# Streaming the activations' high and low halves as one 512-column matmul in a float32 decoder block

## The chip, the cores and the metric

One core of one Trainium2 chip. The metric is device microseconds for one execution of the whole kernel, median over runs.

## The reference, cut to what matters

A decoder block on 256 tokens (S), width 1024 (D): an HGRN2 recurrence and an attention branch read one normalised input, their outputs are projected, gated, summed and projected again, and a SwiGLU FFN (width 2816) follows. All of it is float32.

```python
h = rmsnorm(x, attn_norm_g[l])
proj = h @ w_in[l]
hq, hf, hi, hg, aq, ak, av, gl = jnp.split(proj, IN_SPLITS, axis=-1)
y_hg = hgrn2_mix(hq, hf, hi, hg, lb_all[l], hg_out_norm_g[l]) @ w_branch_hg[l]
...
merged = gates[:, :, 0, :] * y_hg + gates[:, :, 1, :] * y_at
x = x + merged @ w_out[l]
h2 = rmsnorm(x, ffn_norm_g[l])
x = x + (jax.nn.silu(h2 @ w_ffn_gate[l]) * (h2 @ w_ffn_up[l])) @ w_ffn_down[l]
```

## The kernel before, in words

Every large product is done in split precision. A float32 operand becomes a high half in the `fp32r` type, made by a ScalarE copy (line 52), and a low half, the rest, made by a VectorE subtract (line 53); `split` holds the two. A product a x w is then three matmuls: high x high, high x low and low x high, summed in PSUM.

Weights come in parts of 4 k-tiles of 128 rows by 512 columns (1 MB): `load_w` (line 55) issues the DMA on SP's queue and splits what lands. Its three tiles `wraw`, `whi`, `wlo` have three buffers each.

Two helpers do the products with the 1024-wide input. `tok_block` (line 73) keeps the activations stationary and streams 512 weight columns, so tokens lie on partitions and two PSUM banks are used. `feat_block` (line 83) keeps a 128 x 128 weight block stationary and streams the 256 tokens, so features lie on partitions; for each part of 4 k-tiles it goes over 4 feature tiles `ct`, and for each over the 4 k-tiles, with three matmuls of 256 columns (lines 94 to 96). Two feature tiles share one bank of 512 float32 columns, so a block of 512 features takes two banks. Both helpers take their banks from the pool `pw`, which has four; `down` (line 561) accumulates the FFN's last product in four banks of the pools `ph` and `pa`.

In the order of the code: V0 (a token block, its matmuls in lines 137 to 139), F0 (a `feat_block` on columns 1024 to 1535 of `w_in`), then `rx` and `R` (the norm's reciprocal, from the input `xtok` by lines 195, 161, 162; `spread`, line 164, lays it over the partitions with the matmul of line 169), `put_tok(V, V0)` (line 206, empties V0's banks and scales by `rx`), F1, the position bias (line 238 to 257, with copies on POOL in line 253), Q0 and Q1 (`feat_block`, line 261). Then come token blocks for attention between the steps of the recurrence (`hgrn_level`, whose ScalarE copy `KP` in line 296 shares the buffer T15 with the bias' `Bx`), four `feat_block` of branch gates (line 506), two each on `w_at` and `w_hg` (lines 520, 524), a token block on `w_out`, and the FFN: for each 512 hidden features a gate block, an up block and the `down` of the features before.

The Tile framework orders the instructions of each engine when the kernel is built: among those that it holds ready it takes the one written earliest, so an instruction can overtake earlier ones that are not ready in its plan. On the chip each engine then runs in that fixed order. A tile of a pool is given to the next user once all readers of the last one are done.

Of the kernel before, what the change touches and what calls it, by code (L numbers as in the profile page):

```python
# [14 lines left out]
P = 128  # L15
# [3 lines left out]
H = 8  # L19
# [8 lines left out]
def tile_hgrn2_moba_block(ctx: ExitStack, tc: tile.TileContext, xm, xT, vecs, table, onehot,  # L28
# [21 lines left out]

    def split(src, hi, lo):
        nc.scalar.copy(hi, src)  # L52
        nc.vector.tensor_sub(lo, src, hi.bitcast(F32))  # L53
# [19 lines left out]
    def tok_block(w, c0, ah, al, parts=(4, 4)):  # L73
        ps = [pw(), pw()]
        for kt, wh, wl in chunks(w, c0, 512, parts):
            for tb in range(2):
                ts = slice(tb * P, (tb + 1) * P)
                nc.tensor.matmul(ps[tb], ah[:, kt, ts], wh, start=(kt == 0), stop=False)  # L78
                nc.tensor.matmul(ps[tb], ah[:, kt, ts], wl, start=False, stop=False)  # L79
                nc.tensor.matmul(ps[tb], al[:, kt, ts], wh, start=False, stop=(kt == KT - 1))  # L80
        return ps

    def feat_block(w, c0, ah, al, cw=512, parts=(4, 4), cut=1):
        n = cw // P
        ps = [pw() for _ in range(n // 2)]
        k = 0
        for pn in parts:
            hi, lo = load_w(w[k * P:(k + pn) * P, c0:c0 + cw].rearrange("(k p) c -> p k c", p=P), [pn, cw], cut)
            for ct in range(n):
                cs = slice(ct * P, (ct + 1) * P)  # L90
                o = ps[ct // 2].rearrange("p (a t) -> p a t", a=2)[:, ct % 2, :]
                for i in range(pn):
                    kt = k + i
                    nc.tensor.matmul(o, hi[:, i, cs], ah[:, kt, :], start=(kt == 0 and ct % 2 == 0), stop=False)  # L94
                    nc.tensor.matmul(o, hi[:, i, cs], al[:, kt, :], start=False, stop=False)  # L95
                    nc.tensor.matmul(o, lo[:, i, cs], ah[:, kt, :], start=False,  # L96
                                     stop=(kt == KT - 1 and ct % 2 == 1))
            k += pn
        return [p.rearrange("p (a t) -> p a t", a=2) for p in ps]
# [11 lines left out]
    XTh = big.tile([P, KT, S], F32R, name="XTh", tag="XH")  # L111
    XTl = big.tile([P, KT, S], F32R, name="XTl", tag="XL")
    V = big.tile([P, 2, D], F32, name="V", tag="T6")
    V0 = [pw(), pw()]
    for g, pieces in enumerate(((1, 1, 2), (2, 2))):
# [4 lines left out]
        for n in pieces:  # L120
# [6 lines left out]
            for kt in range(xs.start, xs.stop):  # L127
                nc.scalar.mul(XTh[:, kt, :], xTr[:, kt, :], vec[:, kt:kt + 1])
                nc.vector.scalar_tensor_tensor(XTl[:, kt, :], xTr[:, kt, :], vec[:, kt:kt + 1],
                                               XTh[:, kt, :].bitcast(F32), op0=OP.mult, op1=OP.subtract)  # L130
                if kt == xs.start:
                    split(raw[:, ks, :], wh[:, ks, :], wl[:, ks, :])
            for i in range(k0, k0 + n):
                kt = 4 * g + i
                for tb in range(2):
                    ts = slice(tb * P, (tb + 1) * P)
                    nc.tensor.matmul(V0[tb], XTh[:, kt, ts], wh[:, i, :], start=(kt == 0), stop=False)
                    nc.tensor.matmul(V0[tb], XTl[:, kt, ts], wh[:, i, :], start=False, stop=False)
                    nc.tensor.matmul(V0[tb], XTh[:, kt, ts], wl[:, i, :], start=False, stop=(kt == KT - 1))  # L139
# [48 lines left out]
    F0 = feat_block(w_in, 1024, XTh, XTl, cut=2)  # L188
# [22 lines left out]
    K = big.tile([P, 2, H, P], F32, name="K", tag="T2")  # L211
    Fg = big.tile([P, 2, H, P], F32, name="Fg", tag="T3")
    for half in range(2):
        ps = F0 if half == 0 else feat_block(w_in, 1024 + half * 512, XTh, XTl, cut=2 - half)
        for j in range(2):
# [3 lines left out]
            nc.vector.tensor_mul(fz, ps[j].rearrange("p h (b t) -> p h b t", b=2),  # L219
                                 Rb.rearrange("p h (b t) -> p h b t", b=2))  # L220
# [39 lines left out]
    for half in range(2):  # L260
        ps = feat_block(w_in, half * 512, XTh, XTl)
        for j in range(2):
            h = half * 4 + j * 2
            nc.vector.tensor_mul(Q[:, :, h:h + 2, :].rearrange("p b h t -> p h b t"),
                                 ps[j].rearrange("p h (b t) -> p h b t", b=2),
                                 Rqb.rearrange("p h (b t) -> p h b t", b=2))

# [89 lines left out]
    def hgrn_gate(o, ro, sg):  # L357
# [5 lines left out]
        oTh = big.tile([P, H, S], F32R, name="oTh", tag="T3")  # L363
        oTl = big.tile([P, H, S], F32R, name="oTl", tag="T4")
        for g in range(4):
# [6 lines left out]
            hi = oTh[:, 2 * g:2 * g + 2, :].rearrange("p h t -> p (h t)")  # L372
            lo = oTl[:, 2 * g:2 * g + 2, :].rearrange("p h t -> p (h t)")
            nc.scalar.mul(hi, bank, og)
            nc.vector.scalar_tensor_tensor(lo, bank, og, hi.bitcast(F32), op0=OP.mult, op1=OP.subtract)
        return oTh, oTl

# [1 line left out]
    def qk_block(tok, sq, c0, half):  # L379
        put_tok(tok, tok_block(w_in, c0 + half * 512, XTh, XTl), half)  # L380
# [66 lines left out]
    def values(Va, PT0, PT1):  # L447
        aTh = big.tile([P, H, S], F32R, name="aTh", tag="T7")
        aTl = big.tile([P, H, S], F32R, name="aTl", tag="T10")
        for g in range(4):  # L450
# [6 lines left out]
            gs = slice(2 * g, 2 * g + 2)  # L457
            split(bank, aTh[:, gs, :].rearrange("p h t -> p (h t)"), aTl[:, gs, :].rearrange("p h t -> p (h t)"))
        return aTh, aTl
# [15 lines left out]
    put_tok(V, tok_block(w_in, 2048 + 512, XTh, XTl), 1)  # L475
# [3 lines left out]
    put_tok(Va, tok_block(w_in, 6144, XTh, XTl), 0)  # L479
# [3 lines left out]
    put_tok(Va, tok_block(w_in, 6144 + 512, XTh, XTl), 1)  # L483
# [4 lines left out]
    def gate_block(half):  # L488
        ps = tok_block(w_in, 3072 + half * 512, XTh, XTl)
# [4 lines left out]
    aTh, aTl = values(Va, PT0, PT1)  # L494
# [6 lines left out]
    G = []  # L501
    for br in (1, 0):
        g_t = big.tile([P, KT, S], F32, name=f"G{br}", tag=("T5", "T6")[br])
        G.insert(0, g_t)
        for half in range(2):
            ps = feat_block(w_in, 7168 + br * D + half * 512, XTh, XTl)
            for j in range(2):
                g = g_t[:, half * 4 + 2 * j:half * 4 + 2 * j + 2, :]
                nc.vector.tensor_mul(g, ps[j], Rb)
                nc.scalar.activation(g, g, AF.Sigmoid)  # L510
            if br == 1 and half == 0:
                oTh, oTl = hgrn_gate(o, ro, sg)

# [1 line left out]
    Mh = big.tile([P, KT, S], F32R, name="Mh", tag="T8")  # L515
    Ml = big.tile([P, KT, S], F32R, name="Ml", tag="T9")
    x2 = big.tile([P, 2, D], F32, name="x2", tag="T1")
    nc.gpsimd.dma_start(x2, xm.rearrange("(b p) c -> p b c", p=P))
    for half in range(2):
        pa_ = feat_block(w_at, half * 512, aTh, aTl)  # L520
        for j in range(2):
            g = G[1][:, half * 4 + 2 * j:half * 4 + 2 * j + 2, :]
            nc.vector.tensor_mul(g, g, pa_[j])
        pb_ = feat_block(w_hg, half * 512, oTh, oTl)
        for j in range(2):
            ks = slice(half * 4 + 2 * j, half * 4 + 2 * j + 2)
            g = G[0][:, ks, :]
            nc.vector.tensor_mul(g, g, pb_[j])
            nc.vector.tensor_add(g, g, G[1][:, ks, :])
            split(g, Mh[:, ks, :], Ml[:, ks, :])  # L530

# [1 line left out]
    x2h = big.tile([P, KT, S], F32R, name="x2h", tag="XH")  # L533
    x2l = big.tile([P, KT, S], F32R, name="x2l", tag="XL")
    ss2 = small.tile([P, 2, 2], F32, name="ss2")
    for half in range(2):
        ps = tok_block(w_out, half * 512, Mh, Ml)
        for tb in range(2):
# [6 lines left out]
            ks = slice(half * 4, half * 4 + 4)  # L545
            nc.vector.tensor_mul(xg, bank.rearrange("p (k t) -> p k t", k=4),
                                 vec[:, 8 + half * 4:12 + half * 4].unsqueeze(2).to_broadcast([P, 4, P]))
            split(xg, x2h[:, ks, tb * P:(tb + 1) * P], x2l[:, ks, tb * P:(tb + 1) * P])
# [10 lines left out]
    acc = [[None, None], [None, None]]  # L559

    def down(f0, nf, act, last):
        ah, al = act
        for j0 in range(0, nf, 2):
            hi, lo = load_w(w_down[(f0 + j0) * P:(f0 + j0 + 2) * P, :].rearrange("(j p) c -> p j c", p=P), [2, D])
            end = last and j0 + 2 == nf
            for tb in range(2):
                for half in range(2):
                    ts = slice(tb * P, (tb + 1) * P)
                    cs = slice(half * 512, (half + 1) * 512)
                    for i in range(2):  # L570
# [3 lines left out]
                        nc.tensor.matmul(acc[tb][half], ah[:, j, ts], hi[:, i, cs], start=st, stop=False)  # L574
                        nc.tensor.matmul(acc[tb][half], ah[:, j, ts], lo[:, i, cs], start=False, stop=False)  # L575
                        nc.tensor.matmul(acc[tb][half], al[:, j, ts], hi[:, i, cs], start=False, stop=en)  # L576
# [11 lines left out]
    for f0 in range(0, NFT, 4):  # L588
        nf = min(4, NFT - f0)
        pg = feat_block(w_gate, f0 * P, x2h, x2l, cw=nf * P)  # L590
        zt = big.tile([P, 4, S], F32, name="zt", tag=("T12", "T13")[f0 // 4 % 2])
        for j in range(nf // 2):
            z = zt[:, 2 * j:2 * j + 2, :]
            nc.vector.tensor_mul(z, pg[j], R2b)
            nc.scalar.activation(z, z, AF.Silu)
        pu = feat_block(w_up, f0 * P, x2h, x2l, cw=nf * P)
# [53 lines left out]
```

## Time and profile before

| | us |
|---|---|
| median of 3 runs | 516.94 (516.44 to 520.05) |
| the profiled execution, first to last instruction | 514.7 |
| TensorE busy, matmul | 507.1 |
| VectorE busy | 317.4 |
| ScalarE busy | 264.0 |
| POOL busy | 24.7 |

The profiled execution's own time is known as its span, 514.7 us, which lies 2.2 us under the median of the runs. The profile shows one execution. Matmuls overlap, so that the duration of one is longer than the step from its start to the next one's. PE is TensorE, DVE VectorE, ACT ScalarE, POOL GpSimd, SP SyncE. The granted clock of TensorE was 1.00 of full speed in all slices of the page.

### The profile page before, as it was taken

How to read it: one execution, taken by the hardware profiler on the slowest of the kernel's cores; microseconds unless marked ns; L12 is line 12 of the kernel's file. 1: busy time of each engine (PE TensorE's matmuls, PEld its weight loads, DVE VectorE, ACT ScalarE, POOL GpSimd, SP SyncE). 2: the span in 40 equal slices, each digit the busy share in tenths (PEclk: the TensorE clock that was granted, in tenths of full speed). 3: DMA queues.
4: the chain of work that ended last, by engine and by line, in shares of the span. 5: the costliest groups of instructions: out<-in, count | busy, mean ns of one | idle time of the engine just before them, and what ended most of it. 6: DMA issues, size and time to landing. Idle time of an engine off the chain costs nothing.

```text
span 514.7 us, 7998 instructions
## 1 busy us (share of the span) xinstructions
PE 507.1 (99%) x3410; PEld 468.1 (91%) x3410; DVE 317.4 (62%) x314; ACT 264.0 (51%) x355; POOL 24.7 (5%) x42
## 2 busy tenths in 40 slices
PE   7999999999999999999999999999999999999996
PEld 5899988888888889999999988999989899899985
DVE  4769598976698553484556477755544555555362
ACT  5776428787459546954424434644424424443250
POOL 8002250000000000000000000000000000000000
PEclk9999999999999999999999999999999999999999
DMA  7958747526512643185555655555655555653522
GB/s 240 387 193 280 255 165 244 165 81 212 162 46 82 236 165 99 65 265 202 188 164 168 211 195 164 165 171 196 205 165 176 201 196 164 189 179 88 177 105 82
DMA packets 43810, 91.28 MB, mean 177 GB/s; under 512 B 1880, under 2 KB 4472, under 8 KB 43776
## 3 DMA queue, kind: packets, MB, share of 16 engines
q1 hardware_dynamic: 43040, 88.14, 52.0%
q0 software_dynamic: 736, 2.65, 1.6%
q8 instruction: 26, 0.43, 0.3%
q14 instruction: 8, 0.07, 0.0%
HBM read 89.70 MB, written 1.07 MB: 176 GB/s over the span
## 4 chain that ended last, share of the span: by engine, by line
PE 97%; DMA 1%; SPq 0%; DVE 0%; ACT 0%; issue 0%; DVEq 0%
PE pw L96 17%; PE pw L95 17%; PE pw L94 17%; PE pw L78 8%; PE pw L80 8%; PE pw L79 8%; PE acc L576 4%; PE acc L574 4%; PE acc L575 4%; PE ph L302 2%; DMA wraw<-w_in 1%; PE pa L418 1%; PE pa L393 1%; PE ph L345 1%; PE pa L455 1%; PE pw L139 1%
## 5 line engine op out<-in xcount | busy, mean ns | idle before, releaser
L53 DVE TENSOR_TENSOR wlo<-wraw,whi 128x2048 fp32r<-128x2048 f32 (+2 forms) x88 | 190.9, 2171 | 128.9 <-ACT whi L52 128.4
L52 ACT CAST whi<-wraw 128x2048 fp32r<-128x2048 f32 (+2 forms) x88 | 155.4, 1769 | 139.3 <-PE pw L95 46.6
L96 PE MATMUL pw<-x2h,wlo 128*128 128x256 f32 x352 | 99.8, 284 | 0.0
L95 PE MATMUL pw<-x2l,whi 128*128 128x256 f32 x352 | 99.7, 283 | 0.0
L94 PE MATMUL pw<-x2h,whi 128*128 128x256 f32 x352 | 99.6, 283 | 0.0
L94 PE MATMUL pw<-XTh,whi 128*128 128x256 f32 x256 | 72.6, 284 | 0.0
L96 PE MATMUL pw<-XTh,wlo 128*128 128x256 f32 x256 | 72.5, 284 | 0.0
L95 PE MATMUL pw<-XTl,whi 128*128 128x256 f32 x256 | 72.4, 283 | 0.0
L94 PEld LDWEIGHTS pw<-x2h,whi 128*128 128x128 f32 x352 | 67.2, 191 | 0.2
L95 PEld LDWEIGHTS pw<-x2l,whi 128*128 128x128 f32 x352 | 67.2, 191 | 0.2
L96 PEld LDWEIGHTS pw<-x2h,wlo 128*128 128x128 f32 x352 | 67.2, 191 | 0.0
L78 PE MATMUL pw<-whi,XTh 128*128 128x512 f32 x144 | 56.8, 394 | 0.0
L79 PE MATMUL pw<-wlo,XTh 128*128 128x512 f32 x144 | 56.6, 393 | 0.0
L80 PE MATMUL pw<-whi,XTl 128*128 128x512 f32 x144 | 56.4, 392 | 0.0
L96 PEld LDWEIGHTS pw<-XTh,wlo 128*128 128x128 f32 x256 | 49.0, 192 | 0.4 <-DVE R L170 0.4
L94 PEld LDWEIGHTS pw<-XTh,whi 128*128 128x128 f32 x256 | 49.1, 192 | 0.0
L95 PEld LDWEIGHTS pw<-XTl,whi 128*128 128x128 f32 x256 | 49.1, 192 | 0.0
L574 PE MATMUL acc<-whi,ah 128*128 128x512 f32 x88 | 34.3, 390 | 0.0
L575 PE MATMUL acc<-wlo,ah 128*128 128x512 f32 x88 | 34.3, 390 | 0.0
L576 PE MATMUL acc<-whi,al 128*128 128x512 f32 x88 | 34.2, 389 | 0.0
L80 PEld LDWEIGHTS pw<-whi,XTl 128*128 128x128 f32 x144 | 27.0, 188 | 5.6
L78 PEld LDWEIGHTS pw<-whi,XTh 128*128 128x128 f32 x144 | 27.1, 188 | 5.3
(199 smaller groups left out, 743.8 us busy)
## 6 DMA issues: line engine op xcount, KB each, us to landing
wraw<-w_in SPq DMA_DIRECT2D x32, 1024.0 KB, 5.3
wraw<-w_down SPq DMA_DIRECT2D x11, 1024.0 KB, 4.9
wraw<-w_gate SPq DMA_DIRECT2D x10, 1024.0 KB, 5.2
wraw<-w_up SPq DMA_DIRECT2D x10, 1024.0 KB, 5.2
wraw<-w_at SPq DMA_DIRECT2D x4, 1024.0 KB, 5.1
wraw<-w_hg SPq DMA_DIRECT2D x4, 1024.0 KB, 5.4
wraw<-w_out SPq DMA_DIRECT2D x4, 1024.0 KB, 5.0
wraw<-w_in SPq DMA_DIRECT2D x7, 512.0 KB, 8.6
```

The costliest lines, as they stand in the source:

```text
L52: nc.scalar.copy(hi, src)
L53: nc.vector.tensor_sub(lo, src, hi.bitcast(F32))
L78: nc.tensor.matmul(ps[tb], ah[:, kt, ts], wh, start=(kt == 0), stop=False)
L79: nc.tensor.matmul(ps[tb], ah[:, kt, ts], wl, start=False, stop=False)
L80: nc.tensor.matmul(ps[tb], al[:, kt, ts], wh, start=False, stop=(kt == KT - 1))
L94: nc.tensor.matmul(o, hi[:, i, cs], ah[:, kt, :], start=(kt == 0 and ct % 2 == 0), stop=False)
L95: nc.tensor.matmul(o, hi[:, i, cs], al[:, kt, :], start=False, stop=False)
L96: nc.tensor.matmul(o, lo[:, i, cs], ah[:, kt, :], start=False, stop=(kt == KT - 1 and ct % 2 == 1))
L302: nc.tensor.matmul(bank[:, :, i, :], KP[:, h, :], view(QA, h * P + c, [[BS - c, 2], [2 * c, n], [1, c]]), start=True, stop=True)
L574: nc.tensor.matmul(acc[tb][half], ah[:, j, ts], hi[:, i, cs], start=st, stop=False)
L575: nc.tensor.matmul(acc[tb][half], ah[:, j, ts], lo[:, i, cs], start=False, stop=False)
L576: nc.tensor.matmul(acc[tb][half], al[:, j, ts], hi[:, i, cs], start=False, stop=en)
```

## The change

In `feat_block` the activations' high and low halves of one k-tile lie side by side (`[P, 4, 2, S]` for four k-tiles: the tiles `XT`, `oT`, `aT`, `M`, `x2T`, `hT`, in two tiles each where there were separate tiles for high and low), and the high weight block streams both as one matmul of 512 columns. The low weight block streams the high half alone into the first 256 columns of the same bank. One feature tile fills one bank then, and a block of 512 features four. The bank holds two partial sums; `fold` adds them on the way out: a ScalarE copy of the second half to SBUF and a VectorE add of the first half onto it. Where the evacuation read PSUM, it now reads what `fold` wrote, in place or in a new tile `fl` (buffer T15). `hT` alternates between T5 and T6. Token blocks and `down` only address the new layout.

```diff
-    def feat_block(w, c0, ah, al, cw=512, parts=(4, 4), cut=1):
+    def feat_block(w, c0, act, cw=512, parts=(4, 4), cut=1):
         n = cw // P
-        ps = [pw() for _ in range(n // 2)]
+        ps = [pw() for _ in range(n)]
...
             for ct in range(n):
                 cs = slice(ct * P, (ct + 1) * P)
-                o = ps[ct // 2].rearrange("p (a t) -> p a t", a=2)[:, ct % 2, :]
                 for i in range(pn):
                     kt = k + i
-                    nc.tensor.matmul(o, hi[:, i, cs], ah[:, kt, :], start=(kt == 0 and ct % 2 == 0), stop=False)
-                    nc.tensor.matmul(o, hi[:, i, cs], al[:, kt, :], start=False, stop=False)
-                    nc.tensor.matmul(o, lo[:, i, cs], ah[:, kt, :], start=False,
-                                     stop=(kt == KT - 1 and ct % 2 == 1))
+                    both = act[kt // 4][:, kt % 4, :, :].rearrange("p m t -> p (m t)")
+                    if kt > 0:
+                        nc.tensor.matmul(ps[ct][:, 0:S], lo[:, i, cs], part(act, kt, 0), start=False, stop=False)
+                    nc.tensor.matmul(ps[ct], hi[:, i, cs], both, start=(kt == 0), stop=(kt == KT - 1))
+                    if kt == 0:
+                        nc.tensor.matmul(ps[ct][:, 0:S], lo[:, i, cs], part(act, kt, 0), start=False, stop=False)
             k += pn
-        return [p.rearrange("p (a t) -> p a t", a=2) for p in ps]
+        return ps
+
+    def fold(dst, p):
+        if len(dst.shape) == 3:
+            lo, hi = (p[:, m * S:(m + 1) * S].rearrange("p (b t) -> p b t", b=2) for m in range(2))
+        else:
+            lo, hi = p[:, 0:S], p[:, S:2 * S]
+        nc.scalar.copy(dst, hi)
+        nc.vector.tensor_add(dst, lo, dst)
+
+    def flat():
+        return big.tile([P, 4, S], F32, name="fl", tag="T15")
...
-            nc.vector.tensor_mul(fz, ps[j].rearrange("p h (b t) -> p h b t", b=2),
-                                 Rb.rearrange("p h (b t) -> p h b t", b=2))
+            for i in range(2):
+                fold(Fg[:, :, h + i, :], ps[2 * j + i])
+            nc.vector.tensor_mul(fz, fz, Rb.rearrange("p h (b t) -> p h b t", b=2))
...
-                nc.vector.tensor_mul(g, ps[j], Rb)
+                for i in range(2):
+                    fold(g[:, i, :], ps[2 * j + i])
+                nc.vector.tensor_mul(g, g, Rb)
...
+        fl = flat()
+        hT = big.tile([P, 4, 2, S], F32R, name="hT", tag=("T5", "T6")[f0 // 4 % 2])
         for j in range(nf // 2):
             js = slice(2 * j, 2 * j + 2)
-            nc.vector.tensor_mul(zt[:, js, :], zt[:, js, :], pu[j])
-            split(zt[:, js, :], ah[:, js, :], al[:, js, :])
+            for i in range(2 * j, 2 * j + 2):
+                fold(fl[:, i, :], pu[i])
+            nc.vector.tensor_mul(zt[:, js, :], zt[:, js, :], fl[:, js, :])
+            split(zt[:, js, :], hT[:, js, 0, :], hT[:, js, 1, :])
```

The two Q blocks, the projections and the FFN's gate block are changed in the same way as the blocks shown.

## Rows read from the trace of the kernel before

**Rows 1.** The page: busy us, share, instructions; chain that ended last, by engine

```profile
PE 507.1 (99%) x3410; PEld 468.1 (91%) x3410; DVE 317.4 (62%) x314; ACT 264.0 (51%) x355; POOL 24.7 (5%) x42
...
PE 97%; DMA 1%; SPq 0%; DVE 0%; ACT 0%; issue 0%; DVEq 0%
```

**Rows 2.** Groups by line and form: busy us, mean ns, idle before; line 94

```profile
L94 PE MATMUL pw<-x2h,whi 128*128 128x256 f32 x352 | 99.6, 283 | 0.0
L94 PE MATMUL pw<-XTh,whi 128*128 128x256 f32 x256 | 72.6, 284 | 0.0
...
L94 PE MATMUL pw<-aTh,whi 128*128 128x256 f32 x64 | 18.1, 283 | 0.0
...
L94 PE MATMUL pw<-oTh,whi 128*128 128x256 f32 x64 | 18.1, 283 | 0.0
```

**Rows 3.** Timeline of PE, start and us: F0's first and last; a `down` block's

```profile
20.76 0.28 PE L94 MATMUL pw<-XTh,whi 128*128 128x256 f32 x1
...
32.15 0.28 PE L96 MATMUL pw<-XTh,wlo 128*128 128x256 f32 x1
32.27 0.60 PE L169 MATMUL ph<-dg,ones 128*128 128x128 f32 x4
32.63 0.37 PE L94 MATMUL pw<-XTh,whi 128*128 128x256 f32 x1
...
437.91 0.40 PE L574 MATMUL acc<-whi,ah 128*128 128x512 f32 x1
...
448.59 0.39 PE L576 MATMUL acc<-whi,al 128*128 128x512 f32 x1
```

**Rows 4.** Copies out of PSUM: a group by form; VectorE's timeline

```profile
L444 ACT COPY PT<-pa 128x512 f32<-128x512 f32 x6 | 3.3, 611 | 0.0
...
32.91 0.42 DVE L170 COPY R<-ph 128x256 f32<-128x256 f32 x1 [1.76 <-PE ph L169]
```

**Rows 5.** Timelines of ACT and DVE, end of a branch gate block

```profile
236.50 1.90 ACT L52 CAST whi<-wraw 128x2048 fp32r<-128x2048 f32 x1 [3.33 <-issue]
...
238.43 2.29 DVE L53 TENSOR_TENSOR wlo<-wraw,whi 128x2048 fp32r<-128x2048 f32 x1 [3.47 <-ACT whi L52]
240.64 0.68 DVE L509 TENSOR_TENSOR G<-pw,R 128x512 f32<-128x512 f32 x1
242.33 0.69 DVE L509 TENSOR_TENSOR G<-pw,R 128x512 f32<-128x512 f32 x1 [1.01 <-PE pw L96]
```

**Rows 6.** Windows: us, busy (instructions) by engine, granted clock, DMA share, GB/s

```profile
5.00:12.00 7.00, 4.80 (x12) 3.42 (x12) 3.10 (x6) 3.51 (x7) 6.81 (x23) 1.00 0.88 294
...
44.30:56.00 11.70, 11.70 (x100) 11.70 (x99) 11.67 (x16) 5.54 (x5) 4.70 (x4) 1.00 1.00 329
...
254.00:300.00 46.00, 46.00 (x385) 45.96 (x384) 26.59 (x22) 16.94 (x12) 0.00 (x0) 1.00 0.57 184
```

**Rows 7.** Timelines of ACT, DVE and PE around V0's evacuation

```profile
26.94 1.89 ACT L52 CAST whi<-wraw 128x2048 fp32r<-128x2048 f32 x1
28.73 1.26 ACT L206 ACTIVATE V<-pw,rx 128x512 f32<-128x512 f32 x2
...
27.07 0.17 DVE L162 RECIPROCAL rx<-rx 128x2 f32<-128x2 f32 x1 [1.35 <-ACT rx L161]
...
33.29 0.59 PE L238 MATMUL pa<-oh,tb_sb 32*8 32x256 f32 x2
```

**Rows 8.** Timelines of DVE, ACT and POOL in the head

```profile
47.03 0.67 DVE L219 TENSOR_TENSOR Fg<-pw,R 128x512 f32<-128x512 f32 x1
...
50.78 1.91 ACT L52 CAST whi<-wraw 128x2048 fp32r<-128x2048 f32 x1 [1.75 <-PE pw L95]
59.87 1.14 ACT L296 COPY KP<-K 128x1024 f32<-128x1024 f32 x1 [7.17 <-POOL B L253]
...
58.79 1.04 POOL L253 COPY B<-Bx 128x1024 f32<-128x1024 f32 x1 [2.75 <-DMA Bx<-line_d]
```

## What the change will do: the prediction

> **What bounds the kernel now.** I read the profile's busy times and chain first. TensorE is busy 507.1 of 514.7 us and the chain that ends last runs through it for 97% [rows 1]; a microsecond taken from TensorE is a microsecond of the kernel, as long as it doesn't come back as a wait there. Then the groups by line and form: lines 94 to 96, the three matmuls of `feat_block`, run 352 + 256 + 64 + 64 = 736 times each, 2208 matmuls of 256 columns [rows 2]. The mean duration in these rows (283 ns) is latency and not what one costs, since matmuls overlap; the cost is the step from one start to the next, read from the timeline. In the block F0, 96 matmuls start from 20.76 to 32.15 us, 95 steps: 119.9 ns each. In one `down` block, 48 matmuls of 512 columns start from 437.91 to 448.59, 47 steps: 227.2 ns [rows 3]. The two differ by 107.3 ns for 256 columns, so each matmul carries about 12.6 ns that do not depend on its columns (119.9 - 107.3).
>
> **The change part by part.**
>
> *The matmuls.* For each of 736 pairs (feature tile, k-tile) three matmuls of 256 columns become one of 512 and one of 256: 3 x 119.9 = 359.7 ns before, 227.2 + 119.9 = 347.1 ns after, 12.6 ns less. 736 x 12.6 = **9.3 us** off TensorE. No row before shows a 512-column matmul alternating with a 256-column one. The floor of the gain is nothing, if the wide one costs two narrow ones (239.8 ns); the ceiling is 9.3. I take 9.3, since the 512-column row is the same type and width, with a weight load before every matmul as here.
>
> The Trainium skill (TensorE: Matmul & The Clock Gate, "Back-to-back issue gap") gives N / 2.4 + 2.5 ns for a warm matmul, that is 109.2 and 215.8 ns. By it the fixed part would be 2.5 ns and the change would save 736 x 2.5 = 1.8 us. The trace's steps are about 11 ns longer at both widths; the sum goes by the trace.
>
> *The folds.* 92 feature tiles (736 / 8) now leave through a ScalarE copy of 256 columns and a VectorE add of 256. Nearest rows: a ScalarE copy of 512 columns out of PSUM takes 0.61 us, a VectorE copy of 256 out of PSUM 0.42 [rows 4]. I take 0.4 us each (bounds for the copy: 0.3, half of the row, and 0.61): 37 us more on each engine. The multiplications that followed stay, reading SBUF; I cost that change at nothing. ScalarE goes from 264 to about 301 us and VectorE from 317 to about 356 [rows 1]; neither becomes the bound in total. What hides them is TensorE's next matmuls; what it costs when the cover is gone is a wait for a bank, next.
>
> *The banks.* This is the part that speaks against the change. `feat_block` took two of the four `pw` banks, now all four; the next `feat_block` cannot start on a bank before its fold is done. A block lasts 32 x 0.347 = 11.1 us, and its second half finishes one tile every 1.39 us. Tile 0 is finished 3 x 1.39 = 4.16 us before the block ends and its bank is wanted at the end; every other bank has the same 4.16 us. In the branch gates of before, the last half of a block begins with a cast of later weights on ScalarE (236.50, 1.90 us) and their subtract on VectorE (238.43, 2.29 us) [rows 5]. Placed on the new half-block (cast at 0.05 to 1.95 us, subtract at 2.0 to 4.3): tile 0 is done at 1.39, its copy runs behind the cast at 2.0 to 2.4, its add behind the subtract at 4.3 to 4.75; wanted at 5.54. About 0.7 us to spare, more for tiles 1 to 3, whose copies are done by then. So at the 12 tight turns of branch gates, projections and FFN (7 and 5) I cost nothing; VectorE has room there (26.59 of 46 us in the projections [rows 6]). A turn that ends in `down` or in a `tok_block` is not tight: `down` uses other banks. The bound on the other side: an add behind one more 2.35 us subtract comes 1.5 us late at each turn.
>
> *The start.* F0 follows V0 on TensorE, and V0's two banks are emptied by line 206, which waits for `rx`. Before, F0 took the other two banks and did not care. Now tiles 2 and 3 of F0 need V0's. `rx` is ready at 27.07 + 0.17 = 27.24, but ScalarE is by then in a cast (26.94 to 28.83), and V0's two copies run from 28.73 to 29.99 [rows 7]. TensorE has tiles 0 and 1 to run meanwhile: 16 pairs x 0.347 = 5.55 us, from 20.76 to 26.31, if the planned order takes their second half ahead. It can: line 238 stands in the middle of F1's matmuls in the trace though it is written behind them [rows 7]. Tile 2 starts when the first bank is copied: 28.73 + 0.63 = 29.36, a wait of 3.05 us. The 0.36 us of line 169 [rows 3] (its operand comes just after `rx`) moves into that hole: **2.7 us** net. Bounds: if the copy goes as soon as `rx` is there, 27.24 + 0.63 - 26.31 - 0.36 = 1.2 us; if the second half isn't taken ahead, TensorE stands from 20.76 + 8 x 0.347 = 23.54: 5.8 us. I take 2.7, the order of before. No row shows a hole of 3 us; between 5 and 12 us TensorE was busy 4.80 of 7.00 us and the granted clock stayed 1.00 [rows 6], so I add nothing for the clock.
>
> *The head, F1 to Q1.* Three turns with less room. From 44.3 to 56.0 us VectorE is busy 11.67 of 11.70 us [rows 6]; F1's last evacuation started at 47.03 [rows 8], some 2.5 us behind F1's end (32.63 + 96 x 0.12 + 0.5 for line 238 = 44.6). The new deadlines there are 4.16 us, so I take **1.0 us** (bounds 0 and 2.5). And ScalarE: in the trace the copy `KP` (line 296) stands behind the cast of 50.78 and waits for POOL's line 253 until 59.87 [rows 8]; everything behind it on ScalarE stands too. Before, no evacuation of Q was on ScalarE. Now the copies of Q0 are: if they are queued behind `KP`, they come at 61.0. Q0 then ends at about 20.8 + 11.1 x 3 + 2.7 + 0.9 = 57.7; tile 1 of Q1 wants its bank at 59.1 and gets it at 61.0 + 0.4 + 0.4 + 0.2 = 62.0: 2.9 us, or 4.3 if tile 0's copy is behind `KP` as well. If POOL's chain starts earlier (VectorE has less to do at 28 to 33 us than at 34 to 40) or the copies go first, nothing. Between 0 and 4.3 no row decides; I take **1.7 us**.
>
> *The rest* (new tile layout, `hT` in other buffers, `fl`) adds no instruction beside the folds, no DMA and no wait on SP's or POOL's queue; the weight DMAs are issued by the same subtract. The last block ends as before: 10.9 us of `down` cover its folds.
>
> **Sum.** -9.3 + 2.7 + 1.0 + 1.7 = -3.9 us. The span goes from 514.7 to 510.8; the median of the runs lies 2.2 us above the profiled span, so 516.94 - 3.9 = **513.0 us**. About 1% (5.2 us) is what a measurement of this kernel can tell from no change.
>
> **Rivals.**
> - *The start wait is short and all the rest hidden.* Speaks for it: priority for the earlier written V0 copy, the 0.7 us at the steady turns. Against: the cast at 26.94 went first in the trace. 516.9 - 9.3 + 1.2 = 508.8 us.
> - *The turns cost (the other sign).* One mechanism: the add of tile 0 falls behind one more subtract. For it: VectorE and ScalarE run in a fixed order, and the projections with `w_hg` put two folds, two multiplications or adds and a split into each pair. Against: 0.7 us of room as read from the gates. It decides from 6.6 / 15 = 0.44 us of wait per turn over 15 turns (6.6 = 9.3 - 2.7), that is a fold 1.2 us later than I count. At all turns with 1.5 us: 516.9 - 6.6 + 22.5 = 533 us; at half of them 522.
> - *The change doesn't do what it says.* The fixed part belongs to every 256 columns of activations, and the wide matmul costs 239.8 ns: no gain, 516.9 + 5.4 = 522.3 us. Against: [rows 3], where 512 columns pay it once. The Trainium skill's formula (same page and section) lies beside this one: 1.8 us of gain, 520.5 us by it; the rows bear it out at neither width.
> - *The start isn't filled.* TensorE keeps the written order and stands 5.8 us: 513.0 + 3.1 = 516.1 us.
>
> **How the numbers follow.** Forecast 0.59 (its own range 509.8 to 516.5, by the bounds of start and head), short start 0.13, turns cost 0.15, no gain from the width 0.05, start not filled 0.08. Faster by over 1% (below 511.8): 0.13 + about a third of 0.59 = 0.34. Slower by over 1% (above 522.1): most of the turns' 0.15 and half of the 0.05, 0.15. Within 1%: 0.51. The range for 8 in 10 reaches from the short start to the half-way turns: 508.5 to 522.
>
> **What would show it.** Right: steps of 227 and 120 ns alternating in every `feat_block`; 92 copies and 92 adds near 0.4 us; one hole of 2 to 3 us on TensorE between 26 and 30 us, released by the copy of V; at most one more near 58 to 62; none over 0.3 us behind 200. Wrong: a wide matmul near 240 ns; holes at block ends in gates, projections or FFN, put down to VectorE's add; a hole from 23.5 us; a granted clock under 1.00 behind a hole.

## The result, and the profile after

The changed kernel takes 513.5 us, the median of 15 runs (512.12 to 515.68); the kernel before took 516.44 (15 runs, 515.84 to 520.05) beside it. The ratio is 0.9932, 95% interval 0.9916 to 0.9948. The time forecast was 513.0, and the result lies within 1% of it. The change forecast was -3.9 us; the ratio makes it -3.5, the two medians -2.9. The profiled span went from 514.7 to 511.4 us, 3.3 less.

The page of the changed kernel: its span, busy times, the chain that ended last, and groups by line (busy us, mean ns of one). Line 99 is the wide matmul, lines 98 and 101 the narrow one, line 110 the fold's copy. They answer to [rows 1, 2].

```profile
span 511.4 us, 6690 instructions
PE 502.2 (98%) x2674; PEld 427.5 (84%) x2674; DVE 350.9 (69%) x406; ACT 291.8 (57%) x447; POOL 25.4 (5%) x42
...
PE 86%; DVE 6%; ACT 3%; DMA 1%; POOL 1%; issue 1%; SPq 0%; DVEq 0%; POOLq 0%
...
L99 PE MATMUL pw<-x2T,whi 128*128 128x512 f32 x352 | 121.8, 398 | 0.0
...
L98 PE MATMUL pw<-x2T,wlo 128*128 128x256 f32 x308 | 86.6, 281 | 0.0
...
L110 ACT COPY fl<-pw 128x256 f32<-128x256 f32 x38 | 14.0, 370 | 24.9 <-PE pw L99 24.9
```

736 fewer matmuls took only 4.9 us from PE's busy time. The folds cost what was counted: 0.37 us a copy, and the adds 0.42 (the row below), so that ScalarE and VectorE are busy 292 and 351 us where 301 and 356 were forecast. The chain runs less through PE (86%, 97% before) and now passes VectorE and ScalarE on the way.

The fold's adds, by form (ns: smallest, median, largest; first and last start in us):

```profile
L111 DVE TENSOR_TENSOR fl<-pw,fl x38: 409/415/425, 264.2 to 492.9; 128x256 f32<-128x256 f32 x38
```

PE's timeline in an FFN block (start and duration in us), which answers to [rows 3]:

```profile
336.44 0.28 PE L98 MATMUL pw<-x2T,wlo 128*128 128x256 f32 x1
336.56 0.40 PE L99 MATMUL pw<-x2T,whi 128*128 128x512 f32 x1
336.80 0.28 PE L98 MATMUL pw<-x2T,wlo 128*128 128x256 f32 x1
```

From one narrow start to the next is 0.36 us, for a pair forecast at 347 ns. Over all alternating pairs of the trace the mean step behind a narrow matmul is 117.0 ns and behind a wide one 235.1: 352.1 a pair. The narrow one is a little shorter than the 119.9 of before, the wide one 8 ns longer than the 227.2.

So the matmuls give 736 x (359.7 - 352.1) = 5.6 us, not 9.3. Against it stand holes: adding up what every start-to-start step has over the usual one of its widths (steps over it by more than 60 ns) gives 12.4 us before and 15.0 after, 2.6 more. 5.6 less 2.6 is 3.0 of the 3.3 us that the span lost. The largest new holes are 0.25 us at 26.2 to 26.6, 0.7 in three pieces at 33 to 34.5, 0.3 at 58.8, 1.07 at 67.6 and 0.3 at 92.0.

**The start.** Timelines of PE, ACT and DVE around F0's second tile pair, which answer to [rows 7]:

```profile
26.20 0.88 PE L99 MATMUL pw<-XT,whi 128*128 128x512 f32 x2
...
34.13 0.39 PE L101 MATMUL pw<-XT,wlo 128*128 128x256 f32 x1
...
25.70 0.37 ACT L110 COPY Fg<-pw 128x256 f32<-128x256 f32 x1 [3.79 <-PE pw L99]
25.97 1.06 ACT L210 ACTIVATE junk<-xtok 128x1024 f32<-128x1024 f32 x1
...
31.65 1.25 ACT L221 ACTIVATE V<-pw,rx 128x512 f32<-128x512 f32 x2
...
26.11 0.42 DVE L111 TENSOR_TENSOR Fg<-pw,Fg 128x256 f32<-128x256 f32 x1 [2.93 <-ACT Fg L110]
27.42 0.43 DVE L111 TENSOR_TENSOR Fg<-pw,Fg 128x256 f32<-128x256 f32 x1 [0.89 <-ACT Fg L110]
...
31.78 2.29 DVE L56 TENSOR_TENSOR wlo<-wraw,whi 128x2048 fp32r<-128x2048 f32 x1 [1.05 <-ACT whi L55]
```

V0's banks are emptied only at 31.65 to 32.90, yet TensorE goes on at 26.6: F0's tile 2 runs in the bank that F0's own tile 0 has just left (copy at 25.70, add done at 26.53), tile 3 in that of tile 1. (The trace doesn't name the bank; the order of copy, add and next start, and the fixed pairs below, speak for it.) No hole of 2.7 us appears.

But the fold delays what stands behind it on ScalarE. The plan put tile 0's copy ahead of the two squares of `xtok` (line 210) that `rx` needs. ScalarE stood 3.79 us for it, so that they begin at 25.97, though `xtok` had landed at 23.4. In the kernel before they began 2.8 us earlier:

```profile
23.19 1.06 ACT L195 ACTIVATE junk<-xtok 128x1024 f32<-128x1024 f32 x1 [1.52 <-DMA xtok<-xm]
```

With them `rx`, V0's copies (31.65, forecast 28.73) and the split of F1's weights come some 2.9 us later. The largest of the three pieces at 33 to 34.5 is F1's first narrow matmul (34.13), whose weight load waits for the subtract of 31.78. No term of the prediction had this wait.

**The head.** Waits of PE by what ended them (us in total, times, longest), then ACT, DVE and PE where Q1 ends and the first token block follows; they answer to [rows 8]:

```profile
PE pw L81 <- DVE Q L111: 0.8, 1, 0.8
...
61.62 1.14 ACT L314 COPY KP<-K 128x1024 f32<-128x1024 f32 x1 [2.88 <-POOL B L269]
62.83 1.92 ACT L55 CAST whi<-wraw 128x2048 fp32r<-128x2048 f32 x1
64.65 0.37 ACT L110 COPY Q<-pw 128x256 f32<-128x256 f32 x1
...
66.12 2.28 DVE L56 TENSOR_TENSOR wlo<-wraw,whi 128x2048 fp32r<-128x2048 f32 x1
68.33 1.08 DVE L111 TENSOR_TENSOR Q<-pw,Q 128x256 f32<-128x256 f32 x3
...
68.80 0.50 PE L81 MATMUL pw<-whi,XT 128*128 128x512 f32 x1 [0.79 <-DVE Q L111]
```

`KP` (line 314 now) waits for POOL until 61.6, as before. Q0's four copies are ahead of it, so Q0's banks are not late on its account. Q1's may be: the cast of 62.83 and the copy of tile 0 come behind `KP`, and the add of tile 0 then stands behind the subtract of 66.12. The token block's first bank comes free at 68.7. TensorE stands 0.96 us for it, and the step behind is 0.11 us long as well: the 1.07 above.

**The steady turns.** ACT and DVE at the end of a branch gate block, which answer to [rows 5]:

```profile
248.84 1.91 ACT L55 CAST whi<-wraw 128x2048 fp32r<-128x2048 f32 x1 [2.43 <-issue]
250.65 0.36 ACT L110 COPY G<-pw 128x256 f32<-128x256 f32 x1
...
250.78 2.29 DVE L56 TENSOR_TENSOR wlo<-wraw,whi 128x2048 fp32r<-128x2048 f32 x1 [3.09 <-ACT whi L55]
252.99 1.08 DVE L111 TENSOR_TENSOR G<-pw,G 128x256 f32<-128x256 f32 x3
```

This is the turn as it was drawn in the prediction: copy behind the cast, add behind the subtract. Tile 0's bank is free at 253.4, and the next block's first matmul takes it at 254.24: 0.8 us to spare. Behind 200 us no step exceeds its usual one by more than 0.13 us.

### The profile page after: what moved, and what is told of

It is laid out like the page before. It is cut to its first block, busy times and chain, and to the rows that moved or that the text cites. A ratio compares the mean times of both kernels' runs of the same rounds, so it can differ in the third digit from the quotient of the medians.

```text
span 511.4 us, 6690 instructions
## 1 busy us (share of the span) xinstructions
PE 502.2 (98%) x2674; PEld 427.5 (84%) x2674; DVE 350.9 (69%) x406; ACT 291.8 (57%) x447; POOL 25.4 (5%) x42
## 3 DMA queue, kind: packets, MB, share of 16 engines
HBM read 89.70 MB, written 1.07 MB: 178 GB/s over the span
## 4 chain that ended last, share of the span: by engine, by line
PE 86%; DVE 6%; ACT 3%; DMA 1%; POOL 1%; issue 1%; SPq 0%; DVEq 0%; POOLq 0%
PE pw L99 30%; PE pw L98 13%; PE pw L83 6%; PE pw L81 6%; PE pw L82 6%; PE acc L598 4%; PE acc L596 4%; PE acc L597 4%; DVE wlo L56 3%; PE ph L320 2%; PE pw L101 2%; ACT whi L55 2%; DMA wraw<-w_in 1%; POOL qk L295 1%; PE pa L437 1%
## 5 line engine op out<-in xcount | busy, mean ns | idle before, releaser
L99 PE MATMUL pw<-x2T,whi 128*128 128x512 f32 x352 | 121.8, 398 | 0.0
L99 PE MATMUL pw<-XT,whi 128*128 128x512 f32 x256 | 89.6, 399 | 0.0
L98 PE MATMUL pw<-x2T,wlo 128*128 128x256 f32 x308 | 86.6, 281 | 0.0
L99 PEld LDWEIGHTS pw<-x2T,whi 128*128 128x128 f32 x352 | 63.5, 188 | 12.3
L98 PE MATMUL pw<-XT,wlo 128*128 128x256 f32 x224 | 62.8, 281 | 0.0
L98 PEld LDWEIGHTS pw<-x2T,wlo 128*128 128x128 f32 x308 | 58.3, 189 | 1.8
L81 PE MATMUL pw<-whi,XT 128*128 128x512 f32 x144 | 56.9, 395 | 0.8 <-DVE Q L111 0.8
L82 PE MATMUL pw<-wlo,XT 128*128 128x512 f32 x144 | 56.8, 394 | 0.0
L83 PE MATMUL pw<-whi,XT 128*128 128x512 f32 x144 | 56.5, 392 | 0.0
L596 PE MATMUL acc<-whi,hT 128*128 128x512 f32 x88 | 34.3, 390 | 0.0
L598 PE MATMUL acc<-whi,hT 128*128 128x512 f32 x88 | 34.3, 390 | 0.0
L81 PEld LDWEIGHTS pw<-whi,XT 128*128 128x128 f32 x144 | 27.1, 188 | 6.5 <-DVE Q L111 1.1
L83 PEld LDWEIGHTS pw<-whi,XT 128*128 128x128 f32 x144 | 27.0, 188 | 5.6
```

Of the source, the lines that this page charges most:

```text
L81: nc.tensor.matmul(ps[tb], part(act, kt, 0)[:, ts], wh, start=(kt == 0), stop=False)
L82: nc.tensor.matmul(ps[tb], part(act, kt, 0)[:, ts], wl, start=False, stop=False)
L83: nc.tensor.matmul(ps[tb], part(act, kt, 1)[:, ts], wh, start=False, stop=(kt == KT - 1))
L98: nc.tensor.matmul(ps[ct][:, 0:S], lo[:, i, cs], part(act, kt, 0), start=False, stop=False)
L99: nc.tensor.matmul(ps[ct], hi[:, i, cs], both, start=(kt == 0), stop=(kt == KT - 1))
L596: nc.tensor.matmul(acc[tb][half], act[:, j, 0, ts], hi[:, i, cs], start=st, stop=False)
```

## The experiments

Two questions stood open: why the wide matmul takes 235 ns among narrow ones, and what makes the holes. For the first the theories were: a change of width itself costs; writing the same bank twice in turn costs; the folds' traffic at PSUM slows the matmuls; 512 columns cost more in this block whatever surrounds them. For the second: ScalarE's queue behind `KP`, VectorE's backlog, and the banks. The runs of the kernel before that stood beside them had medians of 517.4 to 517.6 us, so the ratios are what to compare.

**Four narrow, then four wide.** For each feature tile and part.

```diff
+                seq = [("n",) + a for a in at] + [("w",) + a for a in at]
+                if k == 0:
+                    seq.insert(0, seq.pop(pn))
```

> The changed kernel with the same matmuls in another order: for each feature tile and part the four narrow matmuls (low weights, 256 columns) stand together and the four wide ones (512) together, in place of one narrow and one wide in turn. Theory A (the wide one costs more only because widths alternate): the step falls from 352.9 ns to about 347 ns for a pair, so 736 x 6 = 4.4 us less, about 509 us. Theory B (a wide matmul that streams activations costs 233 to 235 ns in any order): pairs stay near 352 ns and the time near 513.5 us.

513.71 us (6 runs), ratio 0.9934 [0.9911, 0.9958]. A pair takes 350.3 ns (118.25 + 232.1), between the two theories: 1.8 ns less, 1.3 us for 736 pairs. None of it is seen in the time, since the hole at 67 grew to 2.34 us. ScalarE's timeline of this run tells why:

```profile
64.02 1.12 ACT L316 COPY KP<-K 128x1024 f32<-128x1024 f32 x1 [5.53 <-DVE F L337]
65.05 1.90 ACT L55 CAST whi<-wraw 128x2048 fp32r<-128x2048 f32 x1
66.85 1.18 ACT L112 COPY Q<-pw 128x256 f32<-128x256 f32 x4
```

ScalarE stands 5.5 us in front of `KP`, and all four copies of Q1 come behind it. (The row names VectorE's `F`; POOL's second copy ended at 63.99, and `KP` started at 64.02.)

**Banks and folds alone, all matmuls narrow.** Three matmuls of 256 columns as before, but into halves of a bank of their own.

```diff
+                    nc.tensor.matmul(ps[ct][:, 0:S], hi[:, i, cs], part(act, kt, 0), start=(kt == 0), stop=False)
+                    nc.tensor.matmul(ps[ct][:, S:2 * S], hi[:, i, cs], part(act, kt, 1), start=False, stop=False)
+                    nc.tensor.matmul(ps[ct][:, 0:S], lo[:, i, cs], part(act, kt, 0), start=False, stop=(kt == KT - 1))
```

> The changed kernel with three matmuls of 256 columns again (high x high into the first half of the bank, high x low into the second, low x high into the first), but with one feature tile in a bank and the folds kept. It holds the price of banks and folds alone. If they cost about 2 us, as the holes read from the trace of the changed kernel add up to, and the wide matmul gains 5.2: 516.4 + 2 = 518.5 us, with steps of 120 ns. Rival (folds slow TensorE's steps themselves): steps over 120 ns and a time of 521 us or more.

524.36 us (5 runs), ratio 1.0142 [1.0120, 1.0165]; span 522.4, 7.7 us over the kernel before. The steps are 120.0 to 120.8 ns, so it is not the matmuls: the holes sum to 19.7 us, 7.3 more than before, where 2 were expected. The largest are 1.87 us at 94.3 (no wait for a `pw` bank: TensorE's line 302 waits for VectorE's line 303, itself behind a subtract), 0.93 at 51.9, 0.59 at 34.7, 0.57 at 29.4, 0.54 at 63.4; and most turns of gates, projections and FFN cost 0.1 to 0.25. Such a turn, ACT and DVE:

```profile
247.92 1.91 ACT L55 CAST whi<-wraw 128x2048 fp32r<-128x2048 f32 x1 [0.99 <-PE pw L97]
...
250.27 0.35 ACT L107 COPY G<-pw 128x256 f32<-128x256 f32 x1
...
249.86 2.29 DVE L56 TENSOR_TENSOR wlo<-wraw,whi 128x2048 fp32r<-128x2048 f32 x1 [1.52 <-ACT whi L55]
252.07 0.42 DVE L108 TENSOR_TENSOR G<-pw,G 128x256 f32<-128x256 f32 x1
```

Here the planned order put the last tile's copy behind the cast of the next weights and its add behind their subtract; TensorE wants that bank at 252.36 and gets it at 252.5. This is the rival of the dear turns, small but there. What the banks and folds cost thus depends on the order that the build plans: 7.3 us of holes here, 2.6 in the changed kernel.

**KP's buffer free earlier.** The flipped bias copy goes to T5, so that `KP` needn't wait for POOL.

```diff
-    flip(B1[:, :, P:S], 384 + 128, "T15")
+    flip(B1[:, :, P:S], 384 + 128, "T5")
```

> The changed kernel with the second flipped bias in buffer T5 in place of T15, so that the copy KP on ScalarE does not wait for POOL. The order of all engines but a few instructions stays. Theory (ScalarE standing behind KP delays the last folds of Q, and these hold up the first token block): the hole of 1.0 us on TensorE near 67.6 us shrinks under 0.3, about 512.5 us. Rival (VectorE's own backlog of subtracts makes the hole): the hole stays, 513.5 us.

512.56 us (6 runs), ratio 0.9917 [0.9900, 0.9934], which overlaps the changed kernel's. `KP` now runs at 52.81. The hole at 58.8 is gone, that at 67 is 0.62 where it was 0.96, and not under 0.3. But a second profile of the changed kernel itself (the last run below), where `KP` waits until 62.97, has none at 58.8 either and 0.60 at the turn into the token block. So no part of the hole is shown to come from `KP` in that order. The add of tile 0 still starts at 67.58 behind a subtract of 65.37: that is VectorE's queue.

**All wide.** The low weights stream both halves too, which adds the product low x low that the kernel leaves out.

```diff
+                    nc.tensor.matmul(ps[ct], hi[:, i, cs], both, start=(kt == 0), stop=False)
+                    nc.tensor.matmul(ps[ct], lo[:, i, cs], both, start=False, stop=(kt == KT - 1))
```

> Both weight halves stream both activation halves, two matmuls of 512 columns for each pair (the product of the low halves is added, which the others leave out). No width alternates. Theory A (alternation costs): steps of 227 ns, 453 for a pair, so about 513.5 + 736 x 0.100 = 587 us. Theory B (streaming 512 activation columns costs 235 ns): 470 for a pair, about 600 us.

589.05 us (one run). PE's timeline:

```profile
299.66 0.39 PE L98 MATMUL pw<-oT,wlo 128*128 128x512 f32 x1
299.89 0.39 PE L97 MATMUL pw<-oT,whi 128*128 128x512 f32 x1
300.11 0.39 PE L98 MATMUL pw<-oT,wlo 128*128 128x512 f32 x1
```

The usual step is 226.8 ns, in the same block, with the same banks and folds. So 512 columns of activations cost here what the `down` block showed before, and the extra comes with the mixing of widths.

**Each wide matmul on another bank than the narrow one ahead.** Narrow and wide still alternate, but between two feature tiles. (The narrow one still follows the wide one of its own bank.)

```diff
+                        order = (thin, c), (wide, c + 1), (thin, c + 1), (wide, c)
```

> The changed kernel with wide and narrow matmuls in turn as before, but each on another bank than the one ahead of it (narrow on tile 0, wide on tile 1, narrow on 1, wide on 0; together only at a bank's first and last k-tile). Theory (widths that change cost, whatever the bank): a pair stays near 352 ns. Rival (a wide matmul that adds to a bank of which the narrow one ahead of it has just written half waits for it): a pair falls to 347 ns, the 227 + 120 of uniform rows.

513.78 us (one run). Pairs take 351.8 ns (117.3 + 234.5), as with one bank. So the wide matmul does not pay for the bank that the narrow one has just written.

**A fold without the add.** Only the first half of the bank is copied out, so the product of high weights and low activations is left out of the result.

```diff
-        nc.scalar.copy(dst, hi)
-        nc.vector.tensor_add(dst, lo, dst)
+        nc.scalar.copy(dst, lo)
```

> The changed kernel without the VectorE add of the fold: ScalarE copies the first half of the bank and the second half (high weights x low activations) is left out of the result. Matmuls and banks are as in the changed kernel. Theory (the 92 adds cost only the holes of the head): steps of 352.9 ns for a pair as before, holes at 58.8 and 67.6 us gone, 1 to 2 us less, about 512 us. Rival (the adds' traffic lengthens TensorE's steps): pairs near 347 ns and 4 us less, under 510 us.

514.09 us (4 runs), ratio 0.9938 [0.9919, 0.9957]. Pairs take 352.1 ns (116.9 + 235.2): 92 adds fewer change nothing in the steps. Nor does the time fall, because a hole of 2.0 us opened at 58. ACT, and the PE row that waited:

```profile
58.82 1.09 ACT L313 COPY KP<-K 128x1024 f32<-128x1024 f32 x1 [5.25 <-POOL B L268]
59.81 0.92 ACT L110 COPY Q<-pw 128x256 f32<-128x256 f32 x3
...
60.23 0.50 PE L99 MATMUL pw<-XT,whi 128*128 128x512 f32 x1 [1.85 <-ACT Q L110]
```

Without adds the plan put three of Q0's copies behind `KP`: the place, the culprit and about the size (1.85 us, 1.7 taken) that the prediction gave for `KP`.

**Both at once: four and four, and T5.** The first experiment's order with the third's buffer.

> The grouped kernel (four narrow, four wide in turn) with the flipped bias in T5. Grouping took 2.7 ns from a pair (2 us) and gave it back in a hole of 2.3 us at 67 us. If that hole comes from ScalarE standing behind KP, it goes, about 511 us; if it comes from VectorE's order, it stays, 513.5 us.

510.5 us (5 runs), ratio 0.9873 [0.9852, 0.9894], clear of the first experiment's interval. The pair is 350.2 ns as there (1.8 ns less than alternating, not the 2.7 of the expectation), `KP` runs at 50.63, and the hole of 2.34 us at 67 is gone. Q1's adds start at 67.49, where they started at 69.19 in the first experiment: 1.7 us of that hole was ScalarE's wait for `KP`. The rest isn't seen here because in this execution TensorE comes to the turn 1.3 us later (68.64, 67.32 there).

**Longer groups.** The first half of a block runs 16 wide and then 16 narrow, the second half four and four; T5 again.

```diff
+            if k == 0:
+                for f in (wide, thin):
+                    for ct in range(n):
+                        for i in range(pn):
+                            f(ct, i)
```

> A version from the results so far: widths change as seldom as the banks allow (in a block's first half all 16 wide matmuls, then all 16 narrow; in its second four narrow, four wide for each tile), and the flipped bias in T5. Theory (each change of width costs about 8 ns, grouped or not): 2 changes in the first half and 8 in the second, about 10 x 8 ns in place of 32 x 6.2 a block of 32 pairs, 23 blocks: 2.7 us less than the changed kernel, and 1 us by T5, about 510 us. Rival (TensorE's order moves the holes of the head, as the grouped kernel's hole of 2.3 us at 67 us): 513 us or more.

510.4 us (4 runs), ratio 0.9864 [0.9841, 0.9886]; pairs of 349.2 ns.

**Whole halves.** The second half of the block too: 16 narrow, then 16 wide; T5.

```diff
+            for f in (wide, thin) if k == 0 else (thin, wide):
```

> As the version with seldom changes of width and the bias in T5, but in a block's second half too all 16 narrow matmuls first and then the 16 wide ones, so widths change twice in a block. Theory (wide matmuls cost more for some steps behind narrow ones and then settle at 227 ns): a pair at 347.5 ns in place of 349.2, 1.2 us less, about 509.2 us. Rival (tiles now finish 0.91 us apart, 2.7 us before the next block wants their bank, and the folds don't keep up): holes at the turns of gates, projections and FFN, 511 us or more.

510.43 us (5 runs), ratio 0.9851 [0.9827, 0.9876]. PE's timeline, one row for each unbroken group:

```profile
340.83 7.44 PE L95 MATMUL pw<-x2T,whi 128*128 128x512 f32 x32
348.11 4.00 PE L98 MATMUL pw<-x2T,wlo 128*128 128x256 f32 x32
351.94 0.40 PE L95 MATMUL pw<-x2T,whi 128*128 128x512 f32 x1
```

32 wide ones start in 7.28 us, 227.5 ns each; 32 narrow ones in 3.83, 119.7 each. The first five wide ones behind narrow ones step by 234, 235, 229, 232 and 231 ns, and from then on by 226.7. The pair is 347.4, what the prediction had taken. The wide halves of two blocks meet, so groups are of 32. Groups of 4, of 4 and about 20, and of 32 give 350.2, 349.2 and 347.4 ns, so the extra shrinks with the number of changes, though not in proportion: the first five of a group pay. The time expected, 509.2, was missed; the holes behind 200 us grow by about 1 us over the changed kernel's (the largest 0.25 at 329.6). In time the three can't be told apart (their intervals overlap); all three are faster than before by over 1%.

**The banks in fixed pairs.** This makes the prediction's picture of the start true: V0 holds one pair, F0's tiles 2 and 3 must wait for it.

```diff
+        return psum.tile([P, 512], F32, name=name, tag=("pwA", "pwB")[side], bufs=2)
...
+        ps = [pw(ct // 2) for ct in range(n)]
...
+    V0 = [pw(1), pw(1)]
```

> The changed kernel with the four banks in two fixed pairs: V0 has the second pair, and every block of four feature tiles takes tiles 0 and 1 from the first, 2 and 3 from the second. It makes the prediction's picture of the start true: tile 2 of F0 needs V0's banks. Theory (in the changed kernel tile 2 took the bank that tile 0's fold had freed, and so the start cost 0.25 us in place of 2.7): here TensorE stands from about 26.4 us until V0's first copy, 2.5 to 5.5 us, and the time is 516 us or more. Rival (the start was never in the way): a hole under 0.5 us there, 513.5 us.

518.23 us (one run), span 516.3. PE's timeline, and the window of the start (PE, PEld, DVE, ACT, POOL busy, then the granted clock):

```profile
26.38 0.39 PE L102 MATMUL pw<-XT,whi 128*128 128x512 f32 x1
30.77 0.71 PE L187 MATMUL ph<-dg,ones 128*128 128x128 f32 x4 [4.00 <-DVE dg L186]
31.96 1.65 PE L102 MATMUL pw<-XT,whi 128*128 128x512 f32 x3 [0.48 <-ACT whi L57]
...
20.80:35.00 14.20, 9.72 (x47) 8.03 (x46) 7.30 (x12) 8.11 (x12) 0.00 (x0) 0.88 0.64 235
```

TensorE stands 4 us from 26.6 to 30.8, and behind that wide matmuls step at 427 ns for some 3 us, at the lower of the two clock levels (granted clock 0.50 from 32 to 35 us). The hole exists as soon as the banks are fixed, and then costs more than the 2.7 us counted: the kernel is 4 to 5 us slower than the changed one. The row behind the hole waits for `rx` (line 187 lays it out) and not for V0's copy, which comes at 31.82, 3.1 us later than the prediction took: here too the squares stand behind tile 0's copy. So the hole shows what the lack of a bank costs in this order, not V0's copy alone. What spares the changed kernel, by this comparison, is that the pool gives banks out in the order in which they come free.

**The changed kernel again.**

> The changed kernel itself, beside the others on this chip: 0.993 of the kernel before, about 513.5 us, steps of 352 ns for a pair.

513.99 us (6 runs), ratio 0.9930 [0.9910, 0.9949], pairs of 352.0 ns. This profile differs from the first in the start, below.

## Why the prediction was right or wrong

**The time was right, two terms were wrong in opposite directions.** The matmuls gave 5.6 us instead of 9.3, 3.7 less; the holes cost 2.6 us instead of 5.4, 2.8 less. That the sum came out at 513.0 against 513.5 is partly chance. The range 509.8 to 516.5 isn't what the bounds of start and head add up to, 508.8 to 520.2.

**The matmuls: right in kind, mis-sized.** The step that failed is "I take 9.3, since the 512-column row is the same type and width, with a weight load before every matmul as here". The rows compared uniform stretches; the change makes a mixed one. The runs show 352.1 ns where widths alternate, 347.4 in groups of 32, and 226.7 ns for a wide matmul among its like. The bank that the narrow one wrote (another for the wide one: 351.8) and the adds (none: 352.1) are not the cause. The prediction did say that no row showed the mixture and gave 0 to 9.3 as bounds; a value between them was called for. And the trace before had a hint: the `down` block of [rows 3] follows narrow matmuls. Its start at 437.91 and two rows more:

```profile
439.07 0.39 PE L576 MATMUL acc<-whi,al 128*128 128x512 f32 x1
...
440.20 0.39 PE L575 MATMUL acc<-wlo,ah 128*128 128x512 f32 x1
```

Its first five steps take 1.16 us, 232 ns each, the next five 1.13, 226 each; the mean of 47 hid it. Why a change of width costs some 5 ns a pair is open: no view shows TensorE's inside. A change of width isn't the only thing that brings it: in the all-wide run, behind a wait of 1.2 us at 70.8 among wide matmuls alone, one step of 337 and six of 229 to 235 ns come before 227 is back. The rival that the fixed part belongs to every 256 columns falls.

The formula of the Trainium skill (TensorE: Matmul & The Clock Gate, "Back-to-back issue gap"), which the page gives for an isolated matmul and by which the change would have saved 1.8 us, doesn't hold at these steps: uniform ones are 120.0 and 226.7 ns here, where it gives 109.2 and 215.8.

**The folds: right in size.** 0.37 and 0.42 us for the forecast 0.4 each, hidden in total. What they push back on ScalarE (`rx` by 2.9 us) had no term.

**The start: wrong.** "Now tiles 2 and 3 of F0 need V0's" failed. The prediction read that TensorE would take tiles 0 and 1 through both halves of the weights first, which it did; it did not follow that tile 0 is then folded and its bank free before V0's. Its own rule for banks, that the next user waits until the fold is done, gives exactly this when it is followed tile by tile. The turn to tile 2 costs 0.25 us instead of 2.7. "V0's two copies run from 28.73" failed too, by 2.9 us, and F1 pays for the delay: some 0.4 of its 0.7 us are the wait for its late low weights. The fixed pairs show that the picture would have cost more than 2.7.

**Head turns: half the size, and mostly in another place.** 1.0 + 1.7 us were counted for F1 to Q1, as bank waits between `feat_block`s. Measured are 0.3 us between Q0 and Q1 and 1.07 at the turn into the token block, 1.4 in all. The sentence "A turn that ends in `down` or in a `tok_block` is not tight" holds for `down` only: a token block takes its two banks from the same four and wants the first at once. `KP` as a danger was rightly named: without adds it struck exactly there (1.85 us), and with four and four some 1.7 of 2.34 us, which go when its buffer is freed. In the changed kernel itself no cost of `KP` is shown. Its hole of 67.6 stands behind VectorE's queue, and is 0.62 us with `KP` freed and 0.60 in the second profile with `KP` as it was.

**Steady turns: right**, with 0.8 us to spare where 0.7 was worked out. The rival of dear turns did not occur in the changed kernel. The narrow kernel shows it at 0.1 to 0.25 us a turn, where the planned order was less lucky, so the margin depends on the plan.

**No cost for the clock: right for the changed kernel**, whose hole was too short to matter; a hole of 4 us did bring the lower level, as the fixed pairs show.

## What to carry to other kernels

Cost a mixed sequence of matmuls by a mixed row, look at the first steps behind a change and not at a long mean, or leave room between the bounds: here every change of width took some of the gain, and grouping equal widths gave most of it back. When a block needs more PSUM banks, follow the pool bank by bank, the block's own early tiles among the suppliers, and look at every next user that takes from the same pool. An evacuation moved to another engine joins that engine's queue; search it for an instruction that waits for a slow third engine (here a copy that stood 2.9 to 5.5 us for POOL) and for what it pushes back itself (here `rx`). Widths grouped and the buffer freed together gave 0.985 to 0.987 of the time before; alone, grouping gave 0.993 and the buffer 0.992, about what the change gives without them. Before a small difference of a hole is put down to an edit, profile the unchanged kernel twice: here that alone moved a hole from 0.96 to 0.60 us.

## What the runs showed of the hardware that was not expected

**VectorE and POOL block each other in SBUF.** DVE and POOL of the changed kernel:

```profile
55.17 2.27 DVE L56 TENSOR_TENSOR wlo<-wraw,whi 128x2048 fp32r<-128x2048 f32 x1
57.37 1.52 DVE L283 TENSOR_TENSOR Q<-Q,Rq 128x512 f32<-128x512 f32 x1
...
73.31 6.70 DVE L56 TENSOR_TENSOR wlo<-wraw,whi 128x2048 fp32r<-128x2048 f32 x1
...
56.24 2.10 POOL L269 COPY B<-Bx 128x1024 f32<-128x1024 f32 x1 [4.54 <-DMA Bx<-line_d]
...
71.21 6.64 POOL L295 TENSOR_TENSOR qk<-Q,K 128x2048 f32<-128x2048 f32 x1 [9.63 <-DVE Q L283]
```

The subtract of 73.31 takes 6.70 us, 4.4 more than the usual 2.28, and it overlaps POOL's multiply for 4.5 us (to 77.85). POOL's copy takes 2.10 us, 1.06 more than its shortest of 1.04, and overlaps the subtract of 55.17 for 1.2; the product of 57.37 takes 1.52 instead of 0.68 and overlaps the end of that copy. Each time the later one loses about the overlap. The Trainium skill (SBUF — State Buffer, "Who interferes with whom") states that a VectorE instruction with two SBUF inputs contends with a POOL instruction that reads SBUF; the rows agree. The change bears on it, since the products with `Rq`, which read PSUM before, now read two SBUF operands: two of 1.52 us stand in the full stretch ahead of 67.6. In the second profile both took 0.68 and the hole there was 0.60 us instead of 0.96; that this is the reason was not tested. The prediction costed that change of the products at nothing.

**The clock behind a hole differs between executions of one kernel.** The windows of 9 to 16 us in the first and the second profile of the changed kernel (columns as above):

```profile
9.00:16.00 7.00, 4.52 (x18) 3.08 (x18) 4.36 (x7) 5.24 (x9) 2.91 (x13) 1.00 1.03 377
```

```profile
9.00:16.00 7.00, 4.68 (x14) 3.10 (x14) 4.97 (x9) 5.67 (x9) 2.82 (x13) 0.83 1.05 392
```

In both TensorE stands idle for weights before its matmuls of 12 us, for 2.41 and 2.26 us. In the first it goes on at 227 to 235 ns a step; in the second, from 13.9 to 16.5, at 427, at a granted clock of 0.50, the lower of its two levels (1.2 GHz), and F0 starts 1.4 us later (22.19, 20.83 in the first). A hole of that length may cost nothing or some 1.4 us more than itself. The times differ likewise: of the 15 executions of the changed kernel, the 8 with a mean granted clock of 0.999 or 1.000 have a median span of 510.4 us, the 7 at 0.995 to 0.997 one of 512.4. So small differences between versions are best read at like clocks: with the buffer T5 alone, those at 0.998 or above span 510.3 to 510.6 us, no less than the changed kernel's 510.4.
